# The low part of every fourth weight chunk: minus the rounded weights from ScalarE, the weights added by a transfer from memory

## The chip, the cores and the metric

The kernel runs on one core of one Trainium2 chip. The core has four engines that compute (TensorE for matrix products, VectorE, ScalarE and GpSimd, which the profile calls PE, DVE, ACT and POOL), a fifth that issues transfers (SyncE, SP), and 16 DMA engines that move data between memory and the core's buffers. Each engine works through its own queue of instructions in order and waits on semaphores for the others. The metric is the device time of one execution in microseconds; less is better.

## What is computed

Two layers of a hybrid decoder on 256 positions of width 1024, in float32. Each layer has a half-step SwiGLU feed-forward, a token-mixing sub-layer with three branches, and a second feed-forward:

```python
for l in range(DEPTH):                       # DEPTH = 2, x: (1, 256, 1024)
    x = x + 0.5 * swiglu_ffn(rms_norm(x, ffn1_norm[l]), ffn1_w_in[l], ffn1_w_out[l])   # 1024 -> 2 x 2816 -> 1024
    h = rms_norm(x, mix_norm[l])
    uv, c_q, c_kv, k_rope, z, xbc, dt_raw, gates = jnp.split(h @ w_in[l], IN_OFFSETS, axis=-1)
    y_a = gmlp_mixer(uv, ...)                # gated spatial mixing
    y_b = mla_mixer(c_q, c_kv, k_rope, ...)  # latent attention, 8 heads
    y_c = ssd_mixer(z, xbc, dt_raw, ...)     # convolution and state-space scan
    g = jax.nn.sigmoid(gates)
    merged = sum(g_i * (y_i @ w_branch[l, i]) for i in range(3))
    x = x + merged @ w_out[l]
    x = x + 0.5 * swiglu_ffn(rms_norm(x, ffn2_norm[l]), ffn2_w_in[l], ffn2_w_out[l])
```

Almost all the work is products of activations with weights that are read once: 218 MB of them pass through the core.

## The kernel before

**Weights as a stream of chunks.** The host lays all large weights out in the order of use, in 416 chunks, 208 per layer. A full chunk is a tile of 128 partitions by 1024 float32 values (512 KB); a few in the mixing sub-layer are narrower (828, 768 and 552 columns). Counted from 0, chunks 0 to 65 of a layer belong to the first feed-forward (44 for its input side, four to a group, then 22 for its output), 66 to 141 to the mixing sub-layer (66 to 73 the convolution's input, 74 to 79 the v part, 80 to 92 the rest of the input projection, 93 to 97 the attention's inner projections, 98 to 121 the gates, 122 to 133 the branches, 134 to 141 the output), and 142 to 207 to the second feed-forward, built like the first.

**Each product in three parts.** TensorE multiplies in a rounded format (`F32R`). To keep float32 accuracy, every operand is split into a high part (the value rounded) and a low part (the value minus the high part), and each product is taken as three: high by high, high by low, low by high (`mm3` and `mm3x`, lines 122 to 132). A chunk costs twelve matmuls of 512 columns in the feed-forward, 24 of 256 columns in the convolution's input.

**The life of a chunk.** `load` (line 87) issues the transfer of a chunk into a `raw` tile from SP's queue, with five `raw` tiles in turn. `split` (line 99) makes the parts: ScalarE casts `raw` into `whi` (line 106), then VectorE subtracts, `wlo = raw - whi` (line 107). There are four `whi` and four `wlo` tiles in turn, so that the parts of chunk i take the tiles of chunk i - 4 and can be written only when TensorE has ended that chunk. `next_sub` (line 116) hands a chunk's parts to the stage that uses them, and has the splits run three chunks ahead (`AHEAD = 3`).

**What sets the order.** The program is written in stages, and a scheduler orders each engine's instructions ahead of time; `tc.high_priority()` lets the splits go before other work that is ready. From then on the order in each queue is fixed. Beside the splits, ScalarE applies the activation functions and copies results out of the accumulators, VectorE scales and subtracts, and POOL, idle in the feed-forwards, does in the mixing sub-layer part of the convolution (`tap` and `xbc`, lines 370 and 371), the scan's factors, and the powers for the norms (`rs_...`, line 210). POOL issues no transfers before.

Of the kernel before, what the change touches and what calls it, by code (L numbers as in the profile page):

```python
# [14 lines left out]
AF = mybir.ActivationFunctionType  # L15
ALU = mybir.AluOpType
# [3 lines left out]
P = 128  # L20
# [26 lines left out]
def _specs():  # L47

    ffn = [1024] * (2 * KF) + [1024] * KF
    mix = [1024] * 8 + [828, 828, 552] * 2 + [1024] * 13  # L50
    mix += [768] * 3 + [1024] * 2 + [1024] * 24 + [1024] * 12 + [1024] * KD
    return ffn + mix + ffn
# [9 lines left out]
def tile_trunk(ctx, tc, wst, xtok, xT, pos, pcol, prow, wsT, cst, out):  # L62
    nc = tc.nc
    act, dve, pool, pe = nc.scalar, nc.vector, nc.gpsimd, nc.tensor
# [9 lines left out]
    widths = _specs() * DEPTH  # L74
    starts, o = [], 0
# [4 lines left out]
    raws, splits = {}, {}  # L80
    AHEAD = 3

    def pieces(i):

        return ((0, 512), (512, 1024)) if i == 0 else ((0, widths[i]),)

    def load(n):

        while st["load"] < min(n, len(widths)):
            i = st["load"]  # L90
            w = widths[i]
            r = wp.tile([P, SUB_MAX], F32, name="raw", tag="raw", bufs=5)
            src = wst[starts[i] : starts[i] + P * w].rearrange("(p n) -> p n", p=P)
            for a, b in pieces(i):
                nc.sync.dma_start(out=r[:, a:b], in_=src[:, a:b])
            raws[i] = r
            st["load"] += 1

    def split(i):
        load(i + 1)  # L100
        r = raws.pop(i)
        hi = wp.tile([P, SUB_MAX], F32R, name="whi", tag="whi", bufs=4)
        lo = wp.tile([P, SUB_MAX], F32R, name="wlo", tag="wlo", bufs=4)
        with tc.high_priority():
            for a, b in pieces(i):
                act.copy(hi[:, a:b], r[:, a:b])  # L106
                dve.tensor_tensor(lo[:, a:b], r[:, a:b], hi[:, a:b].bitcast(F32), ALU.subtract)  # L107
        splits[i] = (hi, lo)

    def prefetch(n):  # L110
        i = st["use"]
        while st["split"] < min(i + n, len(widths)):
            split(st["split"])
            st["split"] += 1
# [890 lines left out]
```

## Time and profile before

| | |
|---|---|
| median of 3 runs | 1267.18 us (1265.81 to 1268.96) |
| profiled execution | 1265.58 us |
| its span, first to last instruction | 1263.9 us |
| busy: TensorE, VectorE, ScalarE, POOL | 98%, 63%, 53%, 9% |
| granted TensorE clock | 0.998 |
| read from memory | 219.46 MB, 174 GB/s over the span |

The profile is of one execution. A row of a group has the line of the kernel, the engine, the operation and its tiles (out<-in), the shapes and the count, then busy time, the mean of one in ns, the idle time of the engine just before, and who ended it. A row of a timeline has start and length in us, the same names, and in brackets the idle time before it and its releaser. A row of a table by windows has the window, its length, the busy time of TensorE, its weight loads, VectorE, ScalarE and POOL with their counts, the granted clock, the busy share of the DMA engines and the rate in GB/s.

### The profile page before, as it was taken

The numbers are of one execution on the slowest core, as the hardware profiler recorded it, in microseconds if no ns is written. First come the engines' busy times: TensorE is split into PE (matmuls) and PEld (weight loads), VectorE is DVE, ScalarE is ACT, GpSimd is POOL, SyncE is SP. The second block draws the span as 40 slices with busy tenths as digits, with TensorE's granted clock in tenths as the row PEclk, the third lists the DMA queues.
The fourth block names the chain that finished last, engine by engine and source line by source line (L and its number), as shares of the span: only waits on it lengthen the run. The fifth ranks groups of instructions, "written<-read, shape, count | busy, mean of one in ns | idle before, by whom it ended". The sixth has DMA issues, their size and how long they took to land.

```text
span 1263.9 us, 16711 instructions
## 1 busy us (share of the span) xinstructions
PE 1236.7 (98%) x6332; PEld 1040.2 (82%) x6332; DVE 791.9 (63%) x1097; ACT 667.6 (53%) x908; POOL 119.4 (9%) x108
## 2 busy tenths in 40 slices
PE   8999999999999999999999999999999999999998
PEld 6888889988887778888888888899987877888887
DVE  6555556898756665555556554588895576555553
ACT  7554444647666354454455444456566754555532
POOL 0000003433200000000000000064140000000000
PEclk9999999999999999999999999999999999999999
DMA  8666554534554455555555555535445445555562
GB/s 319 202 183 184 186 192 133 193 124 157 198 172 152 151 172 184 183 185 189 193 180 187 183 183 188 193 116 192 126 159 187 150 151 165 169 185 186 185 189 87
DMA packets 62431, 221.58 MB, mean 175 GB/s; under 512 B 7056, under 2 KB 7184, under 8 KB 62224
## 3 DMA queue, kind: packets, MB, share of 16 engines
q1 hardware_dynamic: 61344, 218.35, 52.5%
q10 hardware_dynamic: 1008, 2.18, 0.5%
q8 instruction: 49, 0.80, 0.2%
q14 instruction: 30, 0.25, 0.1%
HBM read 219.46 MB, written 1.05 MB: 174 GB/s over the span
## 4 chain that ended last, share of the span: by engine, by line
PE 89%; POOL 4%; DVE 3%; issue 1%; ACT 1%; DMA 1%; ACTq 0%; DVEq 0%; POOLq 0%
PE ps_in L131 13%; PE ps_in L130 13%; PE ps_in L132 13%; PE ps_out L132 7%; PE ps_out L130 7%; PE ps_out L131 7%; PE ps_g L132 3%; PE ps_g L131 3%; PE ps_g L130 3%; PE ps_in L126 2%; PE ps_in L124 2%; PE ps_in L125 2%; POOL xbc L371 2%; PE ps_a L269 2%; PE ps_br L130 1%; PE ps_br L131 1%
## 5 line engine op out<-in xcount | busy, mean ns | idle before, releaser
L107 DVE TENSOR_TENSOR wlo<-raw,whi 128x1024 fp32r<-128x1024 f32 (+3 forms) x417 | 513.8, 1235 | 374.2 <-ACT whi L106 373.0
L106 ACT CAST whi<-raw 128x1024 fp32r<-128x1024 f32 (+3 forms) x417 | 431.4, 1039 | 394.1 <-PE ps_in L132 159.5
L130 PE MATMUL ps_in<-whi,xg 128*128 128x512 f32 x704 | 276.6, 396 | 4.2 <-ACT whi L106 3.1
L131 PE MATMUL ps_in<-wlo,xg 128*128 128x512 f32 x704 | 278.9, 396 | 0.5 <-DVE wlo L107 0.5
L132 PE MATMUL ps_in<-whi,xg 128*128 128x512 f32 x704 | 273.5, 391 | 0.0
L130 PEld LDWEIGHTS ps_in<-whi,xg 128*128 128x128 f32 x704 | 131.8, 188 | 36.2 <-ACT whi L106 4.4
L131 PEld LDWEIGHTS ps_in<-wlo,xg 128*128 128x128 f32 x704 | 132.3, 188 | 26.8 <-DVE wlo L107 2.2
L132 PEld LDWEIGHTS ps_in<-whi,xg 128*128 128x128 f32 x704 | 132.0, 188 | 26.2
L124 PE MATMUL ps_in<-xg,whi 128*128 128x256 f32 x336 | 95.5, 287 | 2.8 <-ACT whi L106 1.9
L126 PE MATMUL ps_in<-xg,wlo 128*128 128x256 f32 x336 | 96.3, 287 | 1.5 <-DVE wlo L107 1.5
L125 PE MATMUL ps_in<-xg,whi 128*128 128x256 f32 x336 | 96.1, 287 | 0.0
L131 PE MATMUL ps_g<-wlo,xg 128*128 128x512 f32 x192 | 75.8, 395 | 0.0
L131 PE MATMUL ps_out<-wlo,aa 128*128 128x512 f32 x192 | 75.8, 395 | 0.0
L130 PE MATMUL ps_out<-whi,aa 128*128 128x512 f32 x192 | 75.5, 393 | 0.0
L132 PE MATMUL ps_g<-whi,xg 128*128 128x512 f32 x192 | 75.0, 391 | 0.0
L132 PE MATMUL ps_out<-whi,aa 128*128 128x512 f32 x192 | 74.8, 389 | 0.0
L210 POOL TENSOR_TENSOR rs_x<-ms_x,mhalf 128x2 f32<-128x2 f32 x6 | 4.4, 734 | 729.8 <-DVE ms_x L208 729.8
L130 PE MATMUL ps_g<-whi,xg 128*128 128x512 f32 x192 | 72.7, 394 | 0.0
L124 PEld LDWEIGHTS ps_in<-xg,whi 128*128 128x128 f32 x336 | 64.6, 194 | 4.6 <-ACT whi L106 2.7
L126 PEld LDWEIGHTS ps_in<-xg,wlo 128*128 128x128 f32 x336 | 65.0, 193 | 2.0 <-DVE wlo L107 1.9
L125 PEld LDWEIGHTS ps_in<-xg,whi 128*128 128x128 f32 x336 | 65.0, 193 | 1.1 <-DVE xg L236 0.4
L130 PE MATMUL ps_out<-whi,ab 128*128 128x512 f32 x160 | 62.2, 389 | 0.0
(268 smaller groups left out, 1788.0 us busy)
## 6 DMA issues: line engine op xcount, KB each, us to landing
raw<-in_w SPq DMA_DIRECT2D x397, 512.0 KB, 3.5
raw<-in_w SPq DMA_DIRECT2D x8, 414.0 KB, 3.0
raw<-in_w SPq DMA_DIRECT2D x6, 384.0 KB, 3.0
raw<-in_w SPq DMA_DIRECT2D x4, 276.0 KB, 2.8
x<-in_xT SPq DMA_DIRECT2D x4, 256.0 KB, 6.7
x<-in_x ACTq DMA_DIRECT2D x1, 1024.0 KB, 7.1
out_x<-x ACTq DMA_DIRECT2D x4, 256.0 KB, 3.7
row<-in_prow SPq DMA_DIRECT2D x2, 360.0 KB, 5.6
```

Of the source, the lines that this page charges most:

```text
L106: act.copy(hi[:, a:b], r[:, a:b])
L107: dve.tensor_tensor(lo[:, a:b], r[:, a:b], hi[:, a:b].bitcast(F32), ALU.subtract)
L124: pe.matmul(ps, lhsT=whi, rhs=xhl[:, 0], start=first, stop=False)
L125: pe.matmul(ps, lhsT=whi, rhs=xhl[:, 1], start=False, stop=False)
L126: pe.matmul(ps, lhsT=wlo, rhs=xhl[:, 0], start=False, stop=last)
L130: pe.matmul(ps, lhsT=xhi, rhs=whi, start=first, stop=False)
L131: pe.matmul(ps, lhsT=xhi, rhs=wlo, start=False, stop=False)
L132: pe.matmul(ps, lhsT=xlo, rhs=whi, start=False, stop=last)
L210: pool.tensor_tensor(r, m, mhalf[:, :n], ALU.pow)
L269: pe.transpose(ps[:, i, halves(b)], parts[b][:, P * i : P * (i + 1)], ident)
L371: pool.tensor_tensor(o, o, c, ALU.add)
```

## The change

For every fourth chunk (i % 4 == 3, from chunk 7 on; 103 of 416), `split` takes a new way and returns early. ScalarE writes minus the rounded weights into `wlo`; POOL issues a transfer that reads the chunk from memory once more and adds it to what stands in `wlo`; and ScalarE casts `raw` into `whi` as before. VectorE has no part in such a chunk. The low part is then -rounded(w) + w, the same value as before.

```diff
@@ -101,6 +101,16 @@
         r = raws.pop(i)
         hi = wp.tile([P, SUB_MAX], F32R, name="whi", tag="whi", bufs=4)
         lo = wp.tile([P, SUB_MAX], F32R, name="wlo", tag="wlo", bufs=4)
+        if i > 4 and i % 4 == 3:
+
+            src = wst[starts[i] : starts[i] + P * widths[i]].rearrange("(p n) -> p n", p=P)
+            w = widths[i]
+            with tc.high_priority():
+                act.activation(lo[:, :w], r[:, :w], AF.Copy, scale=-1.0)
+                pool.dma_start(out=lo[:, :w], in_=src, accum_op=ALU.add)
+                act.copy(hi[:, :w], r[:, :w])
+            splits[i] = (hi, lo)
+            return
         with tc.high_priority():
             for a, b in pieces(i):
                 act.copy(hi[:, a:b], r[:, a:b])
```

Lines behind the new ones move by ten: the cast of the other chunks is line 116, their subtraction 117, the three matmuls 134 to 142, POOL's `tap` and `xbc` 380 and 381.

The scheduler places the new instructions. On ScalarE, in the first feed-forward, a group of four chunks before (`s` is the activation of the group that has just ended, `aa` a transposed result):

```order
L298 ACTIVATE s<-ps_in,rs_x 128x256
L106 CAST whi<-raw 128x1024
L298 ACTIVATE s<-ps_in,rs_x 128x256
L106 CAST whi<-raw 128x1024 x2
L270 CAST aa<-ps_a 128x2x256
L106 CAST whi<-raw 128x1024
```

and with the change:

```order
L308 ACTIVATE s<-ps_in,rs_x 128x256
L109 ACTIVATE wlo<-raw 128x1024
L111 CAST whi<-raw 128x1024
L308 ACTIVATE s<-ps_in,rs_x 128x256
L116 CAST whi<-raw 128x1024 x2
L280 CAST aa<-ps_a 128x2x256
L116 CAST whi<-raw 128x1024
```

The negation has come in ahead of the chunk's cast, between the two activations of the group before.

POOL's queue at the end of the first feed-forward and in the convolution of the first layer, before:

```order
L210 TENSOR_TENSOR rs_x<-ms_x,mhalf 128x2
L370 TENSOR_TENSOR tap<-xp,pc 128x256 x2
L371 TENSOR_TENSOR xbc<-xbc,tap 128x256 x2
L370 TENSOR_TENSOR tap<-xp,pc 128x256 x2
L371 TENSOR_TENSOR xbc<-xbc,tap 128x256 x2
```

and with the change:

```order
L110 DMA wlo<-in_w 128x1024 x16
L220 TENSOR_TENSOR rs_x<-ms_x,mhalf 128x2
L380 TENSOR_TENSOR tap<-xp,pc 128x256 x2
L110 DMA wlo<-in_w 128x1024
L381 TENSOR_TENSOR xbc<-xbc,tap 128x256 x2
L380 TENSOR_TENSOR tap<-xp,pc 128x256 x2
L381 TENSOR_TENSOR xbc<-xbc,tap 128x256 x2
```

In the feed-forward POOL has now nothing but transfers to issue; in the convolution a transfer stands behind two taps and ahead of two additions.

POOL's queue where the gates begin (powers and products of the attention's queries and keys), before:

```order
L709 TENSOR_TENSOR qk<-qk,gg 128x8x64
L210 TENSOR_TENSOR rs_k<-ms_k,mhalf 128x16
L210 TENSOR_TENSOR rs_q<-ms_q,mhalf 128x16
L699 TENSOR_TENSOR qk<-qk,rs_k 128x8x64 x2
L359 MEMSET xp 128x2x3 x2
```

and with the change:

```order
L719 TENSOR_TENSOR qk<-qk,gg 128x8x64
L110 DMA wlo<-in_w 128x1024
L220 TENSOR_TENSOR rs_k<-ms_k,mhalf 128x16
L220 TENSOR_TENSOR rs_q<-ms_q,mhalf 128x16
L709 TENSOR_TENSOR qk<-qk,rs_k 128x8x64 x2
L110 DMA wlo<-in_w 128x1024 x7
```

The transfer of chunk 103 stands ahead of the block of powers, that of chunk 107 behind it.

## The prediction

> **What bounds the kernel now.** I read the page first (busy shares, chain), then the groups by shape, then the timeline of ScalarE in the stretches where weights are split.
>
> ```profile
> span 1263.9 us, 16711 instructions
> ...
> PE 1236.7 (98%) x6332; PEld 1040.2 (82%) x6332; DVE 791.9 (63%) x1097; ACT 667.6 (53%) x908; POOL 119.4 (9%) x108
> ...
> PE 89%; POOL 4%; DVE 3%; issue 1%; ACT 1%; DMA 1%; ACTq 0%; DVEq 0%; POOLq 0%
> ```
>
> TensorE is busy for 98% of the span and carries 89% of the chain that ended last; it stands idle for 1263.9 - 1236.7 = 27 us in all. So taking work from VectorE can win little. What it could win is the time in which TensorE waits for a low part made by VectorE:
>
> ```profile
> L131 PE MATMUL ps_in<-wlo,xg 128*128 128x512 f32 x704 | 278.9, 396 | 0.5 <-DVE wlo L107 0.5
> L126 PE MATMUL ps_in<-xg,wlo 128*128 128x256 f32 x336 | 96.3, 287 | 1.5 <-DVE wlo L107 1.5
> L107 DVE TENSOR_TENSOR wlo<-raw,whi 128x1024 fp32r<-128x1024 f32 x397 | 489.8, 1236 | 364.1 <-ACT whi L106 362.8
> L106 ACT CAST whi<-raw 128x1024 fp32r<-128x1024 f32 x397 | 416.1, 1051 | 382.6 <-PE ps_in L132 159.5 <-PE ps_out L132 141.8 <-PE ps_g L132 26.9
> ```
>
> 0.5 + 1.5 = 2.0 us. The last two rows show the split of one chunk, 1.05 us on ScalarE and then 1.24 us on VectorE, and that ScalarE starts it when TensorE gives a buffer back. So the question is whether the new, longer way to a low part still fits between two uses of its buffer.
>
> **The budget of one low part.** In the feed-forward, ScalarE's timeline is a clock of the chunks: a cast starts when TensorE has ended the chunk four earlier.
>
> ```profile
> 102.64 1.05 ACT L106 CAST whi<-raw 128x1024 fp32r<-128x1024 f32 x1 [0.20 <-PE ps_in L132]
> ...
> 111.30 1.05 ACT L106 CAST whi<-raw 128x1024 fp32r<-128x1024 f32 x1 [0.57 <-PE ps_in L132]
> ...
> 148.19 1.05 ACT L106 CAST whi<-raw 128x1024 fp32r<-128x1024 f32 x1 [1.68 <-PE ps_out L132]
> ...
> 156.35 1.05 ACT L106 CAST whi<-raw 128x1024 fp32r<-128x1024 f32 x1 [1.67 <-PE ps_out L132]
> ```
>
> The cast at 102.64 (the last chunk of a group, which is the kind that changes in the first feed-forward) takes a buffer that has just come free; TensorE reaches that chunk three chunks later, at 111.30. Of these 8.66 us, 1.05 go to the new negation on ScalarE, and TensorE's first use of the low part is one matmul (0.23 us) into the chunk. That leaves **7.84 us** from the end of the negation to the landing. Where nothing but weights is done (148.19 to 156.35, 8.16 us; gates, branch and output projections run at the same pace) it is **7.34 us**. Semaphores are a few hundredths (negation to next engine) and left out.
>
> **What the transfer takes.** No accumulating transfer and none from POOL's queue is in this trace. The nearest rows are the loads of the same 512 KB:
>
> ```profile
> q1 hardware_dynamic: 61344, 218.35, 52.5%
> ...
> raw<-in_w SPq DMA_DIRECT2D x397, 512.0 KB, 3.5
> ...
> L95 SPq DMA_DIRECT2D raw<-in_w x417: 327/328/651, 1.2 to 1237.5; - x139
> ...
> DMA to landing us min/median/max: 2.7/3.5/8.3
> ...
> 100.00:180.00 80.00, 80.00 (x365) 65.91 (x364) 43.61 (x47) 38.71 (x49) 0.00 (x0) 1.00 0.59 185
> ```
>
> All loads together take 52.5% of 1263.9 us = 664 us for 218.35 MB, so 0.524 MB moves in 1.6 us; the remaining 1.9 us of the 3.5 is fixed. In the feed-forward the DMA engines are 59% busy with loads already.
>
> - Fixed part: 1.9 us, taken over from the load.
> - Data: the add needs two operands, one from memory and one from the buffer, where a load reads one. Bounds: one stream (1.6 us) and three (both reads and the write in turn, 4.8 us). I take two, 3.2 us, since the reads are what doubles.
> - Sharing with loads: nothing at best, an equal amount again at worst; I take 59% of 3.2 = 1.9 us.
> - Issue on POOL: SP's issue takes 0.33 us, a small POOL operation (a tap) about 1.1. I take the middle, 0.7.
>
> Together **7.7 us**; the bounds are 3.9 (one stream, nothing shared, 0.33 rounded up) and about 12.6 (4.8 + 4.8 + 1.9 + 1.1).
>
> The load's row gives 3.5 us for 512 KB. The Trainium skill, "DMA: Bandwidth & Descriptors", section "Anatomy of one DMA — SWDGE (gpsimd) path", gives a transfer from GpSimd 2.0 us plus its bytes over 436 GB/s, 3.2 us here; its "Collectives: The Full Stack", section on the bandwidth ceiling, lets a reduction read twice per chunk, and with both pages it would be an estimated 4.4 us. No run here shows either yet; by both the transfer would be hidden everywhere, which is a rival below.
>
> **The change part by part.** 103 chunks change (every fourth from the eighth of 416): 65 in the feed-forwards, 38 in the mixing sub-layers.
>
> - VectorE loses 103 subtractions of 1.24 us (128 us) and ScalarE gains 103 passes of 1.05 us (108 us, from 667.6 to about 775 of 1264). Neither is on TensorE's path in the feed-forward: the slot at 102.64 grows by 1.05 us, and the chunk's own cast, which now comes behind the negation, still has 6.5 of its 8.66 us left when it ends. The gain is bounded by the 2.0 us above: **-2 us**. If this cover went, each late pass would cost up to 1.05 us.
> - Feed-forward input chunks, 43: 7.7 against 7.84: **0**.
> - Chunks at the weight-only pace (22 in the feed-forwards' output, 12 gates, 6 branches, 4 output): 44 x (7.7 - 7.34) = **16 us**.
> - Convolution and v part, 8 chunks, where POOL is in the way:
>
> ```profile
> 206.08 1.05 ACT L106 CAST whi<-raw 128x1024 fp32r<-128x1024 f32 x1 [1.82 <-PE ps_in L125]
> 208.96 2.00 ACT L106 CAST whi<-raw 128x1024 fp32r<-128x1024 f32 x2 [1.83 <-PE ps_in L125]
> ...
> 209.86 2.16 POOL L370 TENSOR_TENSOR tap<-xp,pc 128x256 f32<-128x256 f32 x2 [8.23 <-issue]
> ...
> 234.02 0.73 POOL L371 TENSOR_TENSOR xbc<-xbc,tap 128x256 f32<-128x256 f32 x1
> ```
>
> The transfer stands behind two taps, so it starts at 212.02, not at about 210. A chunk takes 2.88 us here (206.08 to 208.96), so TensorE comes to it at 208.96 + 3 x 2.88 = 217.6: 5.6 us are left, 2.1 too few. For all eight at this price, **17 us**.
>
> - The same stage's POOL work, nearly gapless from 209.86 to 234.75 and on the chain, gets three issues more per layer: 6 x 0.7 = **4 us**.
> - The other 8 mixing chunks: the feed-forward's budget, **0**.
> - One gate chunk per layer queues behind POOL's powers:
>
> ```profile
> 319.71 1.05 ACT L106 CAST whi<-raw 128x1024 fp32r<-128x1024 f32 x1 [1.66 <-PE ps_g L132]
> ...
> 321.62 2.48 POOL L699 TENSOR_TENSOR qk<-qk,rs_k 128x512 f32<-128x512 f32 x2
> ...
> 328.79 1.06 ACT L106 CAST whi<-raw 128x1024 fp32r<-128x1024 f32 x1 [1.17 <-PE ps_g L132]
> ...
> 945.18 5.79 POOL L699 TENSOR_TENSOR qk<-qk,rs_k 128x512 f32<-128x512 f32 x2
> ...
> 954.24 1.05 ACT L106 CAST whi<-raw 128x1024 fp32r<-128x1024 f32 x1 [0.86 <-PE ps_g L132]
> ```
>
> POOL is free at 324.10 and 950.97, TensorE comes at 328.79 and 954.24, each plus 0.23: 4.9 and 3.5 us are left, so 2.8 + 4.2 = **7 us**.
>
> Sum: -2 + 0 + 16 + 17 + 4 + 0 + 7 = 42 us. The profiled execution took 1265.58 us (span 1263.9); with 42 it is 1307.6, so **1308 us**. The median of the three runs, 1267.18, is 1.6 above the profiled one, which doesn't matter at this size.
>
> **The rivals.** The transfer's length decides, and the stages go over from "hidden" to "late" at different lengths.
>
> - Late by a little (forecast), 7.2 to 8.8 us: 1287 to 1416 by the same sum. For it: the budget is only twice a load, and a second operand and a second queue must fit. Chance 0.42.
> - Hidden everywhere, not slower than before: the second operand costs nothing beside the first, 3.9 us. The point from which it decides is some 5 us, the room behind POOL's work. Then -2 us, and 6 issues of 0.4 on POOL: 1266 us. For it: the loads' 2.7 us at best, and DMA engines idle for 41% of the feed-forward. Against it: POOL's busy stretches. Chance 0.22, of which 0.06 falls under -0.3%.
> - Hidden in the feed-forward, late in the mixing sub-layer, 5.6 to 7.2 us (at 6.3: 8 x 0.7 + 1.4 + 2.8 + 4 - 2): 1278 us. Chance 0.10.
> - Far too late, the DMA engines as the bound: three streams, 0.7 + 1.9 + 4.8 + 2.8 = 10.2 us: 43 x 2.4 + 44 x 2.9 + 8 x 4.6 + 8 x 2.4 + 12 + 4 - 2 = 300 us, so about 1563. In four chunks the engines would move 4 x 1.6 + 4.8 = 11.2 us of the 11.4 that TensorE needs. For it: the loads' 8.3 us at worst, when the engines are full. Chance 0.26.
>
> **How the numbers follow.** The likeliest case gives 1308. The range goes down to 1262 (hidden, with a gain slightly over the 2.0 us) and up to 1560, the three-stream bound; perhaps 0.03 lies below and 0.1 above. Faster by over 0.3% (about what a measurement can tell from no change, 3.8 us) is 0.06; within 0.3% is the rest of the hidden case, 0.16; slower is 0.42 + 0.10 + 0.26 = 0.78.
>
> **What would show it.** In the page after, TensorE's matmuls that read the low part should show idle time released by a DMA into wlo, tenths of a us at each fourth chunk in output projections and gates and about 2 us at each in the convolution; the issues' table should give the new transfers 7 to 8 us less the issue, and the DMA share in the feed-forward should rise from 0.59 to about 0.59 x 1.5 = 0.88. A landing under 5 us makes "hidden everywhere" right; idle time at every fourth feed-forward chunk of over 2 us, or a share near 1, the last. If TensorE instead waits for whi (ScalarE), the cover that I put over the extra pass is what failed.

## The result, and the profile after

The changed kernel takes 1300.43 us (median, 1293.5 to 1310.16) against 1266.49 us before on the same chip: a ratio of 1.0269 with a 95% interval of 1.0242 to 1.0296, so 34 us slower. The profiled execution of it is the shortest, 1293.5 us, so the profile shows 28 of these 34 us.

The page after, in the parts that answer to those shown of before: the span, the busy shares, the DMA queues, the chain, the groups of the new instructions, and the issues with their time to landing.

```profile
span 1291.8 us, 16916 instructions
...
PE 1246.5 (96%) x6332; PEld 1041.5 (81%) x6332; DVE 674.5 (52%) x994; ACT 762.0 (59%) x1011; POOL 190.2 (15%) x211
...
q1 hardware_dynamic: 61344, 218.35, 49.2%
q0 software_dynamic: 14832, 53.06, 24.8%
...
PE 73%; DMA 14%; DVE 4%; issue 3%; ACT 3%; POOL 3%; ACTq 0%; DVEq 0%; POOLq 0%
...
L110 POOL DMA_DIRECT2D wlo<-in_w x103 | 90.1, 875 | 931.9 <-ACT wlo L109 913.1
L109 ACT ACTIVATE wlo<-raw 128x1024 fp32r<-128x1024 f32 (+2 forms) x103 | 107.5, 1044 | 104.6 <-PE ps_in L141 38.3
...
raw<-in_w SPq DMA_DIRECT2D x397, 512.0 KB, 4.3
wlo<-in_w POOLq DMA_DIRECT2D x97, 512.0 KB, 7.0
```

VectorE has lost 117 us of work and ScalarE has gained 94 (128 and 108 were worked out ahead). TensorE, which carried 89% of the chain, carries 73%; DMA has gone from 1% to 14%. The transfer takes 7.0 us from issue to landing, and the ordinary loads beside it 4.3 instead of 3.5. Who waited for it stands in the view of waits (engine, accumulator and line, what it waited for: us in total, times, longest):

```profile
PE ps_v L141 <- DMA wlo<-in_w: 6.5, 2, 3.6
PE ps_in L136 <- DMA wlo<-in_w: 6.5, 2, 3.4
PE ps_in L141 <- DMA wlo<-in_w: 5.4, 7, 1.3
PE ps_g L141 <- DMA wlo<-in_w: 3.2, 4, 1.1
PE ps_br L141 <- DMA wlo<-in_w: 3.1, 2, 2.0
...
PE ps_out L141 <- DMA wlo<-in_w: 2.1, 3, 1.2
```

26.8 us of waits in 20 places, all in matmuls that read the low part. But 103 chunks changed, and most of them show no wait. Nor is the sum of the waits the loss, though it comes near the 27.9 us by which the span has grown: TensorE's idle time has grown by 18.1 us (from 27.2 to 45.3) and its busy time by 9.8. So some of the waits stand in place of waits that the kernel before has too. The clearest is the wait for VectorE in the scan of the mixing sub-layer, before and after:

```profile
PE ps_sg L458 <- DVE aseg L453: 3.4, 2, 2.3
```

```profile
PE ps_sg L468 <- DVE aseg L463: 0.7, 2, 0.3
```

Where the loss lies can be read without the waits. POOL makes the power for the norm (`rs_x`) once at the start of each of the six sub-layers, and the times from one to the next in POOL's timeline (from the last to the end of the span) divide the execution (before at 12.09, 200.92, 450.78, 637.93, 825.11 and 1076.24; after at 11.92, 203.69, 462.11, 652.37, 842.80 and 1100.27). In us:

| profiled execution | four feed-forwards | two mixing sub-layers |
|---|---|---|
| before | 750.8 | 501.0 |
| after | 764.0 | 515.9 |
| difference | 13.2 | 14.9 |

Two views show how it arises.

In the feed-forward POOL issues one transfer per group of four chunks, so its timeline is a clock of the groups, at two places:

```profile
117.18 0.86 POOL L110 DMA_DIRECT2D wlo<-in_w  x1 [10.69 <-ACT wlo L109]
128.57 0.86 POOL L110 DMA_DIRECT2D wlo<-in_w  x1 [10.52 <-ACT wlo L109]
139.96 0.86 POOL L110 DMA_DIRECT2D wlo<-in_w  x1 [10.52 <-ACT wlo L109]
...
478.41 0.87 POOL L110 DMA_DIRECT2D wlo<-in_w  x1 [11.10 <-ACT wlo L109]
491.52 0.88 POOL L110 DMA_DIRECT2D wlo<-in_w  x1 [12.23 <-ACT wlo L109]
```

Before, the same clock is ScalarE's cast at 102.64 and this one, a group later:

```profile
114.03 1.05 ACT L106 CAST whi<-raw 128x1024 fp32r<-128x1024 f32 x1 [0.20 <-PE ps_in L132]
```

That is 11.39 us, and so are both groups from 117.18 on: nothing is lost there. The group from 478.41 takes 13.11 us, 1.72 more. The time to landing of the single transfers, counted from the start of POOL's issue in the view of the tile, tells the two apart: 7.0 to 7.1 us for the first three rows, 9.0 for the fourth. So there is room for some 7.3 to 7.4 us from the issue (9.0 less 1.72 is 7.3), and a transfer that takes longer delays TensorE by the rest. The wait that TensorE shows in this group is only 1.28 us, so a wait understates what its group loses. The feed-forwards' transfers land in 7.0 us at the median, but 15 of the 65 take over 7.4, up to 9.8, and what they take beyond it is 12.8 us in all, close to the 13.2 of the table.

At the start of the v part, TensorE's rows at the longest wait (first, then two in the middle, then two where the pace changes):

```profile
233.57 0.60 PE L141 MATMUL ps_v<-wlo,xg 128*128 128x276 f32 x1 [3.62 <-DMA wlo<-in_w]
...
234.19 0.43 PE L141 MATMUL ps_v<-wlo,xg 128*128 128x276 f32 x1
234.42 0.43 PE L142 MATMUL ps_v<-whi,xg 128*128 128x276 f32 x1
...
239.16 0.29 PE L142 MATMUL ps_v<-whi,xg 128*128 128x276 f32 x1
239.29 0.29 PE L140 MATMUL ps_v<-whi,xg 128*128 128x276 f32 x1
```

After the wait the matmuls start 0.23 us apart, from 239.02 on 0.13 apart: for 5.4 us TensorE ran at half its clock, which costs 2.7 us more than the wait itself. The same happens behind the wait of 2.87 us at the same place of the second layer (871.89). The table by windows has the first in its column for the granted clock, the third from the end:

```profile
230.00:235.00 5.00, 1.43 (x6) 1.43 (x7) 5.00 (x5) 1.14 (x2) 5.00 (x6) 0.72 0.74 172
235.00:240.00 5.00, 5.00 (x27) 5.00 (x26) 0.77 (x2) 1.72 (x4) 2.89 (x4) 0.60 0.46 125
```

The Trainium skill, "TensorE: Matmul & The Clock Gate", Part 1, says that TensorE falls to half its clock after an idle window of about 3.4 us and recovers after about as long a busy stretch. This trace agrees in the halving, but not in the lengths: in finer windows the granted clock is 1.00 up to 232.20 and 0.50 from there, 2.3 us into the wait of 3.62, and 5.4 us of matmuls pass before it is back. And a wait nearly as long, at chunk 83, is not followed by the half clock at all; its next matmuls start 0.23 and 0.11 us later, and the granted clock is 1.00 throughout:

```profile
257.87 0.39 PE L136 MATMUL ps_in<-xg,wlo 128*128 128x256 f32 x1 [3.35 <-DMA wlo<-in_w]
258.10 0.28 PE L134 MATMUL ps_in<-xg,whi 128*128 128x256 f32 x1
258.21 0.27 PE L135 MATMUL ps_in<-xg,whi 128*128 128x256 f32 x1
```

### The profile page after: what moved, and what is told of

It is laid out like the page before. It is cut to its first block, busy times and chain, and to the rows that moved or that the text cites. A ratio compares the mean times of both kernels' runs of the same rounds, so it can differ in the third digit from the quotient of the medians.

```text
span 1291.8 us, 16916 instructions
## 1 busy us (share of the span) xinstructions
PE 1246.5 (96%) x6332; PEld 1041.5 (81%) x6332; DVE 674.5 (52%) x994; ACT 762.0 (59%) x1011; POOL 190.2 (15%) x211
## 3 DMA queue, kind: packets, MB, share of 16 engines
q0 software_dynamic: 14832, 53.06, 24.8%
## 4 chain that ended last, share of the span: by engine, by line
PE 73%; DMA 14%; DVE 4%; issue 3%; ACT 3%; POOL 3%; ACTq 0%; DVEq 0%; POOLq 0%
DMA wlo<-in_w 13%; PE ps_in L141 11%; PE ps_in L142 11%; PE ps_in L140 11%; PE ps_out L141 6%; PE ps_out L142 6%; PE ps_out L140 6%; PE ps_g L141 2%; PE ps_g L142 2%; PE ps_g L140 2%; PE ps_in L134 2%; PE ps_in L136 2%; PE ps_in L135 2%; PE ps_a L279 1%; ACT wlo L109 1%
## 5 line engine op out<-in xcount | busy, mean ns | idle before, releaser
L117 DVE TENSOR_TENSOR wlo<-raw,whi 128x1024 fp32r<-128x1024 f32 (+3 forms) x314 | 383.8, 1224 | 342.3 <-ACT whi L116 342.0
L116 ACT CAST whi<-raw 128x1024 fp32r<-128x1024 f32 (+3 forms) x314 | 325.6, 1039 | 257.5 <-PE ps_in L142 100.5
L110 POOL DMA_DIRECT2D wlo<-in_w x103 | 90.1, 875 | 931.9 <-ACT wlo L109 913.1
L109 ACT ACTIVATE wlo<-raw 128x1024 fp32r<-128x1024 f32 (+2 forms) x103 | 107.5, 1044 | 104.6 <-PE ps_in L141 38.3
L111 ACT CAST whi<-raw 128x1024 fp32r<-128x1024 f32 (+2 forms) x103 | 104.8, 1017 | 18.0 <-PE ps_in L135 18.0
L310 DVE SCALAR_TENSOR_TENSOR at<-ps_in,rs_x,s 128x256 f32<-128x256 f32 x88 | 42.4, 482 | 55.8 <-ACT s L308 55.8
```

Of the source, the lines that this page charges most:

```text
L109: act.activation(lo[:, :w], r[:, :w], AF.Copy, scale=-1.0)
L110: pool.dma_start(out=lo[:, :w], in_=src, accum_op=ALU.add)
L111: act.copy(hi[:, :w], r[:, :w])
L310: dve.scalar_tensor_tensor(a, ps[b][:, 256:512], rcb, s, ALU.mult, ALU.mult)
```

## The experiments

**Where the loss arises.** Three kernels make the change in some chunks only; the edit is one condition.

```diff
-        if i > 4 and i % 4 == 3:
+        if i > 4 and i % 4 == 3 and not 66 <= i % 208 <= 83:
```

> The ten changed chunks of the convolution, the v part and the first of the middle projection (67, 71, 75, 79, 83 of each layer) are split as before; the other 93 keep the transfer. Theory 1 (the transfer is long everywhere but late mostly here, where POOL stands in its way; its waits of 3 to 4 us also bring the granted clock down): waits of 13 us, some 5 us of slow clock gone, so about 1280 us, ratio 1.011, and a granted clock back at 0.998. Theory 2 (each transfer costs about the same, 34 us over 103): 10 of them give 3 us, about 1297, ratio 1.024.

Measured: 1292.05 us, ratio 1.0199 [1.0174, 1.0223]: 25 us for 93 chunks. It lies between the two expectations, nearer to the second: the chunks left out here (convolution, v part and chunk 83) are not the main cause.

```diff
-        if i > 4 and i % 4 == 3:
+        if i % 4 == 3 and 66 <= i % 208 <= 83:
```

> The other way round: only those ten chunks have the transfer. Theory 1: 15 to 20 us over the kernel before, about 1284 us, ratio 1.014, with the clock below 0.995. Theory 2: 3 us, 1270, ratio 1.003.

Measured: 1276.87 us, 1.0075 [1.0056, 1.0094]: 9.5 us for ten chunks, 0.95 each, between the expected 15 to 20 and 3, so neither theory had it. With the 25 above it makes 34.5: the two parts add up to the whole. The cost of the ten is less than TensorE's waits for them, 11.9 us in this trace; the wait for `aseg` falls here too, from 3.4 to 0.5 us.

```diff
-        if i > 4 and i % 4 == 3:
+        if i > 4 and i % 4 == 3 and not 66 <= i % 208 <= 141:
```

> Only the 65 changed chunks of the feed-forwards have the transfer. Theory 1: the transfer of 7.0 us against a budget of 7.3 to 7.8 us leaves tenths, 6 to 10 us in all, about 1275 us, ratio 1.007. Theory 2: 65 of 103, 21 us, 1288, ratio 1.017.

Measured: 1284.19 us, 1.0132 [1.011, 1.0153]: 17 us for the 65 chunks of the feed-forwards, more than the 6 to 10 of the first theory and under the 21 of the second. Its transfers land in 6.9 us at the median; 16 of the 65 take over 7.4, and what they take beyond it adds up to 16.8 us. By the powers for the norm, as in the table above, its four feed-forwards take 767.7 us, 16.9 more than before: the late transfers are the whole loss there. Eleven of the 16 chunks are among the 15 of the changed kernel, several of them near the start of a feed-forward (7, 143, 151, 351, 359), so being late belongs largely to the place. What is left of the 25, about 8 us, belongs to the 28 other chunks of the mixing sub-layers.

**What in the new way costs.** First the transfer is left out, so that the low part lacks the weights, and all else stays:

```diff
                 act.activation(lo[:, :w], r[:, :w], AF.Copy, scale=-1.0)
-                pool.dma_start(out=lo[:, :w], in_=src, accum_op=ALU.add)
                 act.copy(hi[:, :w], r[:, :w])
```

> All 103 chunks get the negation on ScalarE and lose the subtraction on VectorE, but no transfer is issued (the weights are not added, so the low part is minus the rounded weights). If only the transfer costs: the time of before or up to 2 us less, 1264 to 1267, ratio 0.998 to 1.000. If ScalarE's extra pass of 1.05 us lies on the path: 10 us or more over before, ratio 1.008 or more.

Measured: 1267.82 us, 1.0002 [0.999, 1.0013]. On balance ScalarE's extra pass costs nothing, and taking 120 us of work from VectorE (671.6 busy against 791.9) wins nothing here: the whole loss is the transfer's. Then the transfer overwrites instead of adding, so that the low part is the weights themselves:

```diff
-                pool.dma_start(out=lo[:, :w], in_=src, accum_op=ALU.add)
+                pool.dma_start(out=lo[:, :w], in_=src)
```

> All 103 transfers stay on POOL's queue but don't add (they overwrite the negated weights, so the low part is the weights themselves). If the second operand doubles the data's time, as the sum had it (3.2 + 1.9 shared against 1.6 + 0.9): landing falls from 7.0 to about 4.5 us, the feed-forward's waits go, the DMA share of the feed-forward falls from 0.82 to about 0.72, and the time is about 1272 to 1280 (the conv's queue on POOL stays). If the second operand is free and the length is the queue's: landing stays at 6.5 to 7.0 us and the time at about 1300.

Measured: 1268.01 us, 1.0011 [1.0002, 1.002], faster than either expectation, with a landing between the two. The lines of its page on the new queue and the two kinds of issue:

```profile
q0 software_dynamic: 14832, 53.06, 14.1%
...
raw<-in_w SPq DMA_DIRECT2D x397, 512.0 KB, 4.0
wlo<-in_w POOLq DMA_DIRECT2D x97, 512.0 KB, 6.1
```

The second operand takes the DMA engines' share for the same bytes from 14.1% to 24.8%, 1.76 times as much, yet it makes the landing only 0.9 us longer. These 0.9 us at the median stand between 1 us and 34: at 6.1 the transfer fits in the feed-forwards almost everywhere, and of those there only 2 take over 7.4 us, by 0.6 us in all. And the plain transfer from POOL's queue is already 6.1 us long, 2.1 more than the loads beside it. Last, the add takes its second operand from the `raw` tile on the core, not from memory:

```diff
-                pool.dma_start(out=lo[:, :w], in_=src, accum_op=ALU.add)
+                pool.dma_start(out=lo[:, :w], in_=r[:, :w], accum_op=ALU.add)
```

> All 103 transfers, but the weights are added from the raw tile on the core instead of from memory; the output is the same. If the read from memory makes the transfer long: landing falls from 7.0 to about 6 us and the feed-forward's waits go, 1268 to 1285 us. If both reads cost the same wherever they come from: landing stays near 7 us, and since a raw tile is now held some 7 us longer, loads come later: 1300 us or more, with ScalarE waiting for raw.

Measured: 1267.13 us, 1.0001 [0.9992, 1.001]. The same lines:

```profile
q0 software_dynamic: 14832, 53.06, 21.8%
...
HBM read 219.46 MB, written 1.05 MB: 174 GB/s over the span
...
raw<-in_w SPq DMA_DIRECT2D x397, 512.0 KB, 4.5
wlo<-raw POOLq DMA_DIRECT2D x97, 512.0 KB, 5.4
```

The add stays, the read from memory goes: 1.6 us less to the landing, and the loss is gone. It is the length that counts, not which part of the transfer makes it; in the feed-forwards one transfer is over 7.4, by 0.5. In the v part TensorE still waits 6.1 us for it, and yet the mixing sub-layers take 502.4 us, hardly more than the 501.8 of the kernel without transfers: that one waits 6.0 us for `aseg`, this one 3.2.

**More room.** Five `wlo` tiles in place of four give the low part a chunk more of time. The fifth takes the place of the fifth `raw` tile.

```diff
-            r = wp.tile([P, SUB_MAX], F32, name="raw", tag="raw", bufs=5)
+            r = wp.tile([P, SUB_MAX], F32, name="raw", tag="raw", bufs=4)
...
-        lo = wp.tile([P, SUB_MAX], F32R, name="wlo", tag="wlo", bufs=4)
+        lo = wp.tile([P, SUB_MAX], F32R, name="wlo", tag="wlo", bufs=5)
```

> Five tiles for the low part instead of four, and four instead of five for the raw chunk to make room. If the wait is for the budget between two uses of a low tile: one chunk (2.7 us) more of it hides the transfer in the feed-forward and most of it elsewhere, 1270 to 1285 us, provided that ScalarE's queue lets the negation start earlier. If the wait is for POOL's queue in the convolution alone: waits there stay, about 1290. If four raw tiles starve the split: slower than 1300, with ScalarE waiting for a DMA into raw.

Measured: 1281.49 us, 1.0134 [1.0106, 1.0162]: half the loss goes, with the transfer at 7.8 us, even longer than before. The time is in the first expectation, its reason is not: the transfer isn't hidden in the feed-forwards, which take 758.8 us, 8 more than in the kernel before, and TensorE still waits 12.8 us for the low part (26.8 with four tiles). ScalarE's negation now waits 10.5 us in all for loads. How much of the rest comes from the fewer `raw` tiles and how much from the longer transfer is open, since four `raw` tiles were not tried by themselves.

**POOL's queue in the convolution.** The prediction blamed the taps that stand ahead of the transfer on POOL. Here they go to VectorE, with the transfer in the ten chunks of the second experiment only:

```diff
-                    if b == 0:
+                    if b <= 1:
```

> As e2_only_conv (ten transfers, all in the convolution, the v part and the first middle chunk), with POOL's taps moved to VectorE, so that POOL has nothing in front of these transfers. To be compared with e8_before_dve_taps. If POOL's queue makes the transfers late: the distance to e8 falls from 9.5 us (e2 to before) to about 4 us, and the wait of the v part's chunk (3.4 us in e2) goes. If it is the transfer's length alone: the distance stays at 9 us.

Its mark is the kernel before with the same edit:

> The control: the kernel before with the same taps on VectorE and no transfer. VectorE gets 24 operations of 0.82 us more in the convolutions, where it is busy for 71% of the time, and POOL's chain, which bounds the stage before, goes: within 5 us of before, 1262 to 1272 us.

Measured: 1272.56 us, 1.0047 [1.0031, 1.0064], and for the mark 1259.95 us, 0.9943 [0.9928, 0.9958]. The ten transfers cost 12.6 us beside it, not less than the 9.5 with POOL's taps. So the queue alone is not the cause. The edit to the kernel before by itself makes it 7 us faster, more than expected.

Four kernels show the first changed chunk of the v part (75 of the first layer). In the changed kernel the negation on ScalarE (223.69, to 224.58), then POOL's issue:

```profile
227.60 0.87 POOL L110 DMA_DIRECT2D wlo<-in_w  x1
```

It comes 3.0 us after the negation, behind POOL's taps and additions, and lands 5.9 us later; TensorE is 3.6 us late. With the taps on VectorE, POOL's and TensorE's rows:

```profile
223.52 0.86 POOL L110 DMA_DIRECT2D wlo<-in_w  x1 [3.48 <-ACT wlo L109]
...
231.46 0.39 PE L141 MATMUL ps_v<-wlo,xg 128*128 128x276 f32 x1 [3.36 <-DMA wlo<-in_w]
```

Issued at once (0.29 us after the negation), it lands only after 7.9 us, and TensorE is 3.4 us late all the same. The table by windows says with what it now coincides: the DMA engines, idle in 222 to 224, are full while it runs, and four loads are issued from 0.2 us ahead of it to its end (223.3, 224.6, 228.1 and 230.2), where the changed kernel issues one during its transfer (231.3) and one 1.7 us ahead of it (225.9).

```profile
222.00:224.00 2.00, 2.00 (x19) 2.00 (x18) 0.91 (x3) 2.00 (x4) 0.48 (x1) 1.00 0.00 0
224.00:226.00 2.00, 2.00 (x18) 2.00 (x18) 2.00 (x5) 2.00 (x4) 0.50 (x2) 1.00 0.87 225
226.00:228.00 2.00, 2.00 (x17) 1.88 (x15) 2.00 (x5) 1.80 (x4) 0.00 (x0) 1.00 0.98 179
228.00:230.00 2.00, 0.10 (x1) 0.00 (x0) 2.00 (x5) 0.56 (x1) 0.00 (x0) 1.00 1.06 328
```

That the loads make it long is likely, but not shown: the engines are 0.88 to 0.92 busy during the shorter transfer too.

With the add from the `raw` tile and the taps still on POOL (the kernel of 1267.13 us above):

```profile
225.61 0.87 POOL L110 DMA_DIRECT2D wlo<-raw  x1
...
229.76 0.57 PE L141 MATMUL ps_v<-wlo,xg 128*128 128x276 f32 x1 [2.84 <-DMA wlo<-raw]
```

The transfer is short, 4.1 us, but issued 3.7 us after the negation, and TensorE is 2.8 us late. Last, both at once: the taps on VectorE and the add from `raw`, in the ten chunks.

```diff
-        if i > 4 and i % 4 == 3:
+        if i % 4 == 3 and 66 <= i % 208 <= 83:
...
-                pool.dma_start(out=lo[:, :w], in_=src, accum_op=ALU.add)
+                pool.dma_start(out=lo[:, :w], in_=r[:, :w], accum_op=ALU.add)
...
-                    if b == 0:
+                    if b <= 1:
```

> The ten transfers of the convolution and v part alone, POOL's taps on VectorE, and the add made from the raw tile on the core. Nothing is left out. With the taps alone moved, the first v chunk's transfer started 3 us sooner and still came 3.3 us late, landing in 7.7; with the raw tile as source alone it landed in 4.2 but was issued 3.7 us after the negation, behind the taps, and came 2.8 to 3.3 us late. Theory 1: the room there is about 4 us, and POOL's queue and the transfer's length each use it up by themselves; with both gone TensorE's wait for ps_v falls from 6.6 us to under 1, and the time is 0.994 to 0.997. Theory 2: the order of TensorE's matmuls alone makes the part late whatever the transfer takes; the wait stays at 4 or more, and the time at 1.000 or over.

Measured: 1265.36 us, 0.9984 [0.9974, 0.9993]. Issued at once (222.33) and landing in 5.0 us, the transfer is now 0.6 us late; from the view of waits:

```profile
PE ps_v L141 <- DMA wlo<-raw: 1.2, 2, 0.6
```

So the wait went nearly as the first theory said, from 6.6 to 1.2 us, with nearly the same order of TensorE's matmuls ahead of it. The time did not go as either said: it is 5 us above the mark. In the trace time is lost behind the scan's wait for VectorE, by the windows of this kernel:

```profile
888.00:892.00 4.00, 2.03 (x7) 1.86 (x8) 3.24 (x6) 2.74 (x6) 1.41 (x2) 0.70 0.33 102
892.00:896.00 4.00, 4.00 (x18) 3.82 (x18) 2.56 (x6) 2.13 (x4) 1.05 (x2) 0.50 0.23 72
```

A wait of 2.29 us for `aseg` ends at 889.97, and the clock falls to 0.70 and 0.50: 1.2 + 2.0 = 3.2 us. In the mark the same wait is 1.50 us in this layer (882.24), and the clock stays at 1.00. In the first layer both kernels have the half clock, behind 2.38 us here and 1.91 in the mark. How much of the 5 us this explains is open: the profiled execution is the slowest of the ten, 1268.83 us, and whether the others had the same half clock isn't known. Why the wait grew was not tried.

**What is left of the gain.** The transfers where they are hidden, from the `raw` tile, not in chunks 66 to 83, and the taps on VectorE, beside the kernel before with the taps moved, once more:

```diff
-        if i > 4 and i % 4 == 3:
+        if i > 4 and i % 4 == 3 and not 66 <= i % 208 <= 83:
...
-                pool.dma_start(out=lo[:, :w], in_=src, accum_op=ALU.add)
+                pool.dma_start(out=lo[:, :w], in_=r[:, :w], accum_op=ALU.add)
...
-                    if b == 0:
+                    if b <= 1:
```

> The add is made from the raw tile on the core (landing about 5.4 us, below the 6.2 at which it was hidden), not in chunks 66 to 83 of a layer, and POOL's two taps per block are on VectorE. Nothing is left out. Theory 1: VectorE's relief is worth nothing in this kernel, since TensorE waits for VectorE only 2.0 us in all; the time is that of the taps on VectorE alone, ratio 0.994, within 0.002 of the next kernel. Theory 2: VectorE, now with more to do in the mixing sub-layer, gives back more when it is relieved there: 0.990 or less, 5 us under the next kernel. A ratio over 0.998 would say that the transfers still cost 5 us or more in the gates and branches.

> The kernel before with the taps on VectorE, once more beside the kernel above: 0.994 again (0.9928 to 0.9958 was measured). Both theories expect the same of it; it is the mark for the other.

Measured: 1257.26 us (1256.65 to 1257.75), 0.9919 [0.9904, 0.9934], and the mark 1260.10 us (1258.57 to 1261.59), 0.9942 [0.9925, 0.9958]. The two do not overlap: 2.8 us, between the two expectations. The gain lies in the mixing sub-layers, 491.4 us against the mark's 495.3; the feed-forwards lose 1.1. In the view of waits of the mark, and then of the new kernel, the wait for VectorE in the output projection of the mixing sub-layer is halved:

```profile
PE ps_out L132 <- DVE ma L271: 2.4, 2, 1.2
```

```profile
PE ps_out L142 <- DVE ma L281: 1.2, 2, 0.6
```

This is the fastest kernel of the study, 10 us below the kernel before; 7 of them come from the taps alone.

## Why the prediction was right, and where its sum was not

Slower by 34 us was forecast as slower by 42: the likeliest case, "late by a little". Its terms were less good than their sum, and luck has a part in it. By its length, 7.0 us, the transfer isn't in that case (7.2 to 8.8) but in the rival "hidden in the feed-forward, late in the mixing sub-layer" (5.6 to 7.2 us, some 1278 us, chance 0.10); and that rival is wrong as well, since half of the loss lies in the feed-forwards. No case had a transfer that is short enough at the median and late in one chunk of four.

- **The transfer**: 7.0 us at the median against 7.7, by two errors that partly cancel. A plain transfer from POOL's queue would have been 1.9 + 1.6 + 0.9 + 0.7 = 5.1 us by the prediction's terms and took 6.1; the second operand would have been 2.6 (1.6 of data and its part of the sharing) and added 0.9. The Trainium skill, "DMA: Bandwidth & Descriptors", section "Anatomy of one DMA — SWDGE (gpsimd) path", gives 3.2 us for the plain transfer; measured beside the loads it is nearly twice that. The DMA share in the feed-forward rose to 0.83, with 0.88 forecast:

```profile
100.00:180.00 80.00, 79.96 (x363) 65.31 (x361) 35.52 (x39) 44.28 (x54) 6.05 (x7) 1.00 0.83 233
```

- **VectorE's relief**, -2 us: nothing with the whole change less its transfers, 2.8 us where the transfers come from `raw`, spare chunks 66 to 83, and the taps are on VectorE in both kernels. The size came out near, but by luck: the 2.0 us were waits for `wlo`, and the one wait that the view shows clearly shorter is that for `ma`, by 1.2; the rest of the 2.8 is not traced.
- **The feed-forward**, 0 for the 43 input chunks and 8 for the 22 output chunks: 17 measured. This is the step that failed most: "7.7 against 7.84: **0**" for the input chunks, where the feed-forwards alone have 13.8 of their 16.8 us beyond 7.4; the output chunks, forecast at 8, have 3.0. The room was nearly right: 7.4 from the issue and 0.29 from ScalarE to POOL (the negation at 104.28 ends at 105.34, POOL issues at 105.63), which had been "left out". What was wrong is to set one length against it. The median passes; one transfer in four does not, and the loss is the sum of what those are late. The output chunks' 8 us failed the other way: most of them show no wait, where tenths at each were expected.
- **Convolution and v part**, 17, and POOL's issues, 4: 9.5 measured for the ten chunks from 67 to 83. The mechanism was half right. POOL's queue does hold the transfer back by 3 us, but taking it away gains nothing: the transfer then lands 2 us later after its issue, while more loads run beside it. The room is short: about 4.4 us from the issue (in the last of the four kernels from 222.33 to 226.76, when TensorE begins to wait), since TensorE's order there has 17 of chunk 72's 24 matmuls ahead of the last 22 of chunk 71, which frees the tile, and the v chunks have 18 matmuls. Either the queue or the length uses it up; only with both gone was the chunk nearly in time. That eight chunks each lose 2.1 us was wrong: the waits are 13 us in four places, 6.5 us at chunk 75 of each layer and 6.5 at chunk 83, which the prediction has among "the other 8 mixing chunks", at 0; and part of the 13 only replaces the wait for `aseg`.
- **Gates, branches, the rest**, 8 + 0 + 7: about 8 measured. The powers on POOL were not tried apart. In the trace they hold back a transfer in the first layer only, which is issued 1.6 us after its negation and makes TensorE wait 0.98 us; 2.8 and 4.2 were forecast.
- **Left out altogether**: the half clock after some waits of TensorE, 2.7 us in each of the two places named above.

With the measured 7.0 in place of 7.7 the prediction's own sum would have come to some 20 us (nothing in the feed-forward, 8 x 1.4 in the convolution, 6 x 0.87 of issues, 2.1 + 3.5 behind the powers, less 2). A transfer taken too long and a spread not taken at all have come out near the truth together.

The rival "hidden everywhere" was one step away: at 6.1 or 5.4 us the same kernel takes the time of before. The point from which that happens, put at 5 us, lies between 6.1 and 7.0. "Far too late" is excluded by the landing and by a share of 0.83.

## What to carry to other kernels

Moving work off an engine that is not on the path pays what the path waited for it, here 0 to 3 us for some 120 us of work, while the detour is held against the room between two uses of a buffer: work out that room with every hop in it, from the release of the tile to the first use, before the busy shares. Set the spread of the transfer's time against it, not the median: 0.9 us more at the median moved a quarter of the feed-forwards' transfers over the limit, and that was half of the loss. Don't take the sum of the waits for the loss either: a wait may replace another, and the time of each stage says what was lost. And where a transfer is late behind a queue, look at what runs beside it if it is early; the source on the core was worth more here than the earlier issue.

## What the hardware showed unexpectedly

- An accumulating transfer of 512 KB takes 1.76 times the DMA engines' share of a plain one from the same queue (24.8% against 14.1% of the span for 53.06 MB), but takes only 1.15 times as long to land (7.0 against 6.1 us). With its source on the core it takes 5.4 us.
- A plain transfer from POOL's queue took 6.1 us where a load of the same size from SP's queue took 4.0 in the same execution.
- Some waits of TensorE are followed by some 5 us at half clock, so that they cost nearly double, and others of the same length are not. In the changed kernel those of 3.62 and 2.87 us were, those of 3.35 and 3.13 (895.96) were not; in the kernel with the taps on VectorE 3.28 (857.66) was and 3.36, shown above, was not; 2.25 (263.58) was not in the kernel before, and 1.91 (260.39) was in the mark. So the length of the wait alone does not decide. Several of those that were are shorter than the 3.4 us of the Trainium skill's section named above ("TensorE: Matmul & The Clock Gate", Part 1).
- The times of the changed kernel spread over 1.3% (1293.5 to 1310.16), those of before over 0.3%. Why some transfers are long was not settled. They are partly the same chunks in two kernels (11 of 15 and 16). The loads beside them don't tell them apart: at 1209.47 a transfer lands in 6.9 us with loads issued 1.8 us before and 0.6 and 4.3 after its issue, at 1092.17 one lands in 9.8 with 1.6 before and 0.6 and 4.6 after. The last one, at 1277.03, has no load beside it and takes 5.4.
